# Seven-product matrix groups: two snapshots and a subtraction written ahead of the next group's parts, at high priority

## The chip, the cores and the metric

The kernel runs on one core of a Trainium2 chip. The metric is the device time of one execution in microseconds. The five engines of the core work at the same time, each through a queue of its own and in the order of that queue: PE (TensorE, matrix products, with its weight loads shown apart as PEld), DVE (VectorE), ACT (ScalarE), POOL (GpSimd, here mostly an issuer of transfers) and SP (an issuer of transfers). A difference of up to 0.3% is what a measurement of this kernel cannot tell from no change.

## The reference

Two layers, each with one norm, one wide input projection, three parallel mixers (a short convolution, stick-breaking attention, gated linear attention, GLA), a gate on each, and one output projection into the residual stream. `x` is 512 tokens by 2048.

```python
def _layer(x, norm_g, w_in, ...):
    h = _rmsnorm(x, norm_g)
    proj = h @ w_in                       # 2048 x 7696
    y_conv = _short_conv(cv_h, cv_b, cv_c, conv_w, conv_b) * silu(cv_g)
    y_sb = _stick_breaking(q, k, v) * silu(sb_g)
    y_gla = _rmsnorm(_gla(gl_q, gl_k, gl_v, g), gla_on_g) * silu(gl_g)
    mix = concatenate([y_conv, y_sb, y_gla])
    return x + mix @ w_out                # 2048 x 2048
```

## The kernel before

**Groups of 256 columns.** The weights of both projections are taken in 76 groups of 256 columns, in a fixed order (`specs`). A group is loaded into a staging tile `st` (two of them), its scale is found from squares (ACT, L383, then POOL, L399), and it is split into a high and a low half-precision part: ACT writes the high part `wh` (L507 or L454), DVE writes the low part `wl` (L508 or L461). A product of two split numbers is three half-precision products: high by high, high by low, low by high.

**Seven products instead of eight.** 42 of the groups are "quick": `wsums` (L512 on) cuts the group's weights into two by two blocks, forms sums of blocks, and splits seven of them (the last has the names `w7h`, `w7l`). `project_quick` then needs seven block products instead of eight, a Strassen scheme of Winograd's form. The seven products (`prod`, each 24 matmuls of 128x256 where the result has columns of the projection in partitions, L793, or 48 of 128x128 where it has tokens in partitions, L796) accumulate in four half banks `pa`, `pb`, `pd`, `pf`. Some accumulators are read in the middle of the work: `pa` is copied to `y12` after the first product (ACT, L808) and goes on accumulating with the fifth; `pb` minus that copy goes to `y21` (DVE, L809) before `pb` takes the sixth; `pd` is copied to `y22` (ACT, L812) before the seventh. These three readings are called the first snapshot, the first subtraction and the second snapshot here. The product that next writes the accumulator waits for its reading, and PE's queue is in order, so all of PE waits with it.

**Who sets the order.** ACT and DVE carry, beside the readings, the splits of the *next* group, the elementwise work of attention and GLA, and the squares of the group after. A scheduler of the framework lays out each engine's queue ahead of time, from the order in which the code is written and from a time line of its own; work inside `tc.high_priority()` is preferred to other ready work. The splits of the next group are made by `hook(...)`, which calls `parts_of` (L487 on), and `parts_of` runs inside `tc.high_priority()`. `hook` is called after the second product. The readings have no such mark, so a ready split is preferred to a ready reading.

**Staging.** The load of the group after next into a staging tile (POOL, L362) waits until the last split of the tile's old group, `w7l`, is made on DVE.

Of the kernel before, what the change touches and what calls it, by code (L numbers as in the profile page):

```python
# [10 lines left out]
AF = mybir.ActivationFunctionType  # L11
ALU = mybir.AluOpType
# [31 lines left out]
def hybrid_trunk(ctx, tc, x, norm_g, w_in, conv_w, conv_b, sb_qn_g, sb_kn_g,  # L44
                 gla_w_up, gla_b_up, gla_on_g, w_out, out):
    nc = tc.nc
    V, S, G, T = nc.vector, nc.scalar, nc.gpsimd, nc.tensor
# [27 lines left out]
    def sm(n, tag, bufs=None):  # L75
        return small.tile([P, n], F32, tag=tag, name=nm(tag), bufs=bufs or 1 + (tag in TWICE))
# [7 lines left out]
    def bank(pool, tag):  # L84
        return pool.tile([P, 512], F32, tag=tag, name=nm("ps" + tag))
# [402 lines left out]
    def hook(mm):  # L488

        if hooks:  # L490
            hooks.pop(0)(mm)
# [44 lines left out]
    def weights():  # L536

        i = cursor[0]
        cursor[0] += 1
        held = names[i][:2] == "v " or names[i] == "conv h 1"  # L540
        if i + 2 < len(specs) and not held:
            with tc.high_priority():
                fetch(i + 2)
        assert not hooks

        def first(mm):
            squares(i + 1, mm)
            if held:
                with tc.high_priority():
                    fetch(i + 2, added[0])  # L550

        if i and i + 1 < len(specs):
            hooks.extend([first, lambda mm: parts_of(i + 1, mm)])
        return loaded.pop(i)
# [130 lines left out]
    for l in range(depth):  # L685
# [92 lines left out]
        def project_quick(src, sums, y, cols):  # L778

            (w11, wT2, w22, wT3, w21, wt1, wT4), u = weights()  # L780
            (pa, pb), (pd, pf) = ([bk[:, n * GW:(n + 1) * GW] for n in range(2)]
                                  for bk in [bank(psp, "p") for _ in range(2)])
            a11, a12, a22 = ([a[:, 2 * r:2 * r + 2, c::2, :] for a in src] for r, c in ((0, 0), (0, 1), (1, 1)))
            s_, a21_22, a12_s, a11_21 = sums

            def prod(o, w, a, start, stop=False):
                for t in range(1 if cols else 2):
                    for kk in range(HK):
                        for i, (p_, q_) in enumerate(((0, 0), (0, 1), (1, 0))):
                            st_ = start and t == kk == i == 0  # L790
                            en = stop and kk == HK - 1 and i == 2
                            if cols:
                                mm = T.matmul(o, w[q_][:, kk, :], a[p_][:, :, kk, :], start=st_, stop=en,  # L793
                                              skip_group_check=True)
                            else:
                                mm = T.matmul(o[:, t * P:(t + 1) * P], a[p_][:, t, kk, :], w[q_][:, kk, :], start=st_,  # L796
                                              stop=en, skip_group_check=True)
                            if start and t == kk == 0 and i == 2 and o is pa:
                                hook(mm)
                return mm  # L800

            y11, y12, y21, y22 = (
                y[:, c, r * GW:(r + 1) * GW] if cols else y[:, 2 * r:2 * r + 2, c * P:(c + 1) * P]
                for r in range(2) for c in range(2))
            za, zb, zd, zf = (a if cols else a.rearrange("p (t c) -> p t c", c=P) for a in (pa, pb, pd, pf))
            prod(pa, w11, a11, True)
            hook(prod(pb, wT2, s_, False))
            S.activation(y12, za, AF.Copy)  # L808
            V.tensor_tensor(y21, zb, y12, ALU.subtract)  # L809
            prod(pf, w22, a12_s, True)  # L810
            prod(pd, wT3, a11_21, False)
            S.activation(y22, zd, AF.Copy)  # L812
            prod(pa, w21, a12, False)
            prod(pb, wt1, a21_22, False, True)
            S.activation(y11, za, AF.Copy)
            V.tensor_tensor(y12, zb, y12, ALU.subtract)
            V.tensor_tensor(y22, y12, y22, ALU.subtract)
            lastmm[0] = prod(pd, wT4, a22, False, True)
            V.tensor_tensor(y12, zf, y12, ALU.add)
            yield 0, u  # L820
            V.tensor_tensor(y21, zd, y21, ALU.subtract)
            yield 2, u
# [70 lines left out]
        def mixscale(j, m, tag, top=11.0):  # L893

            pow2(pmix[:, j:j + 1], m, -top, tag)
            s_ = sm(1, tag + "smix")
            V.reciprocal(s_, pmix[:, j:j + 1])
            return s_
# [103 lines left out]
        for tag in ("qT", "kT"):  # L1002
# [10 lines left out]
            s_ = sm(1, "gas")  # L1013
# [300 lines left out]
        for j in range(4):  # L1314
# [17 lines left out]
            s_ = mixscale(2 + j, m, "b", 12.0)  # L1332
# [141 lines left out]
```

## Time and profile before

| what | value |
|---|---|
| median of 3 runs | 1646.34 us (1645.41 to 1650.85) |
| profiled execution | 1652.09 us, of which the span of the profile is 1650.3 us |
| PE busy | 1624.0 us (98%) |
| DVE busy | 1418.1 us (86%) |
| ACT busy | 1184.7 us (72%) |
| weight loads (PEld) busy | 1342.5 us (81%) |
| POOL busy | 265.8 us (16%) |

A row of a time line has the start, the time (both in us), the engine, the line of the kernel, the operation, and `out<-in` by the names of the tiles; in brackets stands the idle time of the engine before it and what ended it. In the view of waits a row has the total, the number of times and the longest. A matmul's shown time is from its issue to a modelled end, and matmuls overlap, so the pace of PE is read from starts.

### The profile page before, as it was taken

The numbers are of one execution on the slowest core, as the hardware profiler recorded it, in microseconds if no ns is written. First come the engines' busy times: TensorE is split into PE (matmuls) and PEld (weight loads), VectorE is DVE, ScalarE is ACT, GpSimd is POOL, SyncE is SP. The second block draws the span as 40 slices with busy tenths as digits, with TensorE's granted clock in tenths as the row PEclk, the third lists the DMA queues.
The fourth block names the chain that finished last, engine by engine and source line by source line (L and its number), as shares of the span: only waits on it lengthen the run. The fifth ranks groups of instructions, "written<-read, shape, count | busy, mean of one in ns | idle before, by whom it ended". The sixth has DMA issues, their size and how long they took to land.

```text
span 1650.3 us, 41605 instructions
## 1 busy us (share of the span) xinstructions
PE 1624.0 (98%) x17914; PEld 1342.5 (81%) x17914; DVE 1418.1 (86%) x2377; ACT 1184.7 (72%) x1743; POOL 265.8 (16%) x298
## 2 busy tenths in 40 slices
PE   8999999999999999999999999999999999999999
PEld 6746668989999967799986468689898989668998
DVE  7977989989898978898699689898898889888893
ACT  7667887877777776756766687787777768666571
POOL 0121011111112121111112011221121111211110
PEclk9999999999999999999999999999999999999999
DMA  7144334486768687544633344445776886894441
GB/s 259 54 146 127 73 113 100 116 161 149 166 148 167 148 167 207 161 154 150 204 110 116 103 116 112 132 94 137 152 157 153 151 163 152 165 189 157 154 155 53
DMA packets 193913, 234.90 MB, mean 142 GB/s; under 512 B 90226, under 2 KB 154044, under 8 KB 193216
## 3 DMA queue, kind: packets, MB, share of 16 engines
q0 software_dynamic: 76992, 177.22, 40.5%
q1 hardware_dynamic: 107728, 45.56, 14.5%
q10 hardware_dynamic: 9008, 9.45, 1.7%
q8 instruction: 140, 2.29, 0.6%
q14 instruction: 45, 0.37, 0.1%
HBM read 179.65 MB, written 14.68 MB: 118 GB/s over the span
## 4 chain that ended last, share of the span: by engine, by line
PE 37%; DVE 6%; DMA 4%; ACT 2%; issue 1%; POOL 0%; SPq 0%; DVEq 0%; ACTq 0%; POOLq 0%
PE psp L796 10%; PE psp L793 6%; PE psp L843 5%; PE psp L712 3%; PE psp L714 3%; PE psp L713 3%; PE psp L701 2%; PE psp L702 2%; PE psp L703 2%; DMA st<-in_w_in_dram 2%; DVE wl L508 1%; DMA m<-mixd 1%; DMA th<-za 1%; DVE za L1280 1%; DMA kT<-raw 1%
## 5 line engine op out<-in xcount | busy, mean ns | idle before, releaser
L507 ACT ACTIVATE wh<-st,ws 128x1024 f16<-128x1024 f32 x252 | 280.8, 1145 | 174.5 <-DVE st L527 92.0
L508 DVE SCALAR_TENSOR_TENSOR wl<-st,ws,wh 128x1024 f16<-128x1024 f32 x252 | 316.7, 1278 | 31.1 <-ACT wh L507 31.0
L383 ACT ACTIVATE junk<-st 128x2048 uint8<-128x2048 f32 x150 | 285.4, 1903 | 17.9 <-DMA st<-in_w_in_dram 8.8
L793 PE MATMUL psp<-s,wh 128*128 128x256 f16 x1152 | 195.6, 273 | 0.0
L793 PEld LDWEIGHTS <-wh 128*128 128x128 f16 x1728 | 168.3, 98 | 21.5 <-issue 1.3
L796 PE MATMUL psp<-wh,s 128*128 128x128 f16 x2048 | 176.9, 219 | 1.9 <-issue 1.9
L714 PE MATMUL psp<-wh,m 128*128 128x256 f16 x640 | 174.5, 273 | 1.2 <-DVE m L1189 1.2
L712 PE MATMUL psp<-wh,m 128*128 128x256 f16 x640 | 174.5, 273 | 0.2 <-issue 0.2
L796 PEld LDWEIGHTS <-s 128*128 128x128 f16 x3072 | 172.9, 98 | 2.0 <-issue 2.0
L713 PE MATMUL psp<-wl,m 128*128 128x256 f16 x640 | 174.5, 273 | 0.0
L796 PE MATMUL psp<-wl,s 128*128 128x128 f16 x1024 | 173.2, 219 | 0.0
L461 DVE SCALAR_TENSOR_TENSOR wl<-st,ws,wh 128x2048 f16<-128x2048 f32 x68 | 158.9, 2346 | 14.6 <-ACT wh L454 13.8
L454 ACT ACTIVATE wh<-st,ws 128x2048 f16<-128x2048 f32 x66 | 130.5, 1995 | 40.7 <-DVE ws L415 22.6
L362 POOL DMA_DIRECT2D st<-in_w_in_dram x114 | 109.8, 1029 | 297.8 <-DVE w7l L508 110.7
L793 PE MATMUL psp<-s,wl 128*128 128x256 f16 x576 | 156.7, 273 | 0.0
L796 PEld LDWEIGHTS <-m 128*128 128x128 f16 x2304 | 131.1, 98 | 2.7 <-issue 2.2
L399 POOL PARTITION_ALL_REDUCE wgm<-wm x75 | 55.5, 740 | 482.5 <-ACT junk L383 469.4
L386 POOL DMA_DIRECT2D st<-st x34 | 54.0, 1589 | 307.2 <-ACT junk L383 266.8
L793 PEld LDWEIGHTS <-wl 128*128 128x128 f16 x864 | 84.5, 98 | 13.4 <-issue 3.4
L796 PE MATMUL psp<-wh,m 128*128 128x128 f16 x1024 | 91.5, 219 | 0.4 <-DVE kT L809 0.4
L796 PE MATMUL psp<-wl,m 128*128 128x128 f16 x512 | 87.5, 219 | 0.0
L703 PEld LDWEIGHTS <-wl 128*128 128x128 f16 x448 | 43.8, 98 | 53.6 <-DVE wl L461 2.3
(442 smaller groups left out, 4199.8 us busy)
## 6 DMA issues: line engine op xcount, KB each, us to landing
st<-in_w_in_dram POOLq DMA_DIRECT2D x114, 1024.0 KB, 8.3
st<-in_w_out_dram POOLq DMA_DIRECT2D x32, 1024.0 KB, 8.5
st<-st POOLq DMA_DIRECT2D x34, 512.0 KB, 6.8
st<-in_w_in_dram SPq DMA_DIRECT2D x6, 1024.0 KB, 12.0
mixd<-g POOLq DMA_DIRECT2D x20, 256.0 KB, 7.9
x<-in_x_dram SPq DMA_DIRECT2D x4, 1024.0 KB, 4.9
qT<-in_x_dram ACTq DMA_DIRECT2D x8, 512.0 KB, 6.2
qT<-xs ACTq DMA_DIRECT2D x8, 512.0 KB, 4.0
```

The lines of the kernel that those rows point to most:

```text
L362: load = queue.dma_start(s_, src[l, h * HK * P:(h + 1) * HK * P, c0:c0 + GW].rearrange("(k p) n -> p k n", p=P), max_dma_last_dim=1024)
L383: sq = S.activation(junk(HK * GW).rearrange("p (k n) -> p k n", k=part.shape[1]), part, AF.Square, accum_out=peak[i][:, h:h + 1])
L454: hi = S.activation(wh[:, :, :GW], staged[i][h], AF.Copy, scale=scales[i])
L461: V.scalar_tensor_tensor(wl[:, :, :GW], staged[i][h], scales[i], wh[:, :, :GW], ALU.mult, ALU.subtract)
L507: hi = S.activation(h_, b, AF.Copy, scale=sc)
L508: V.scalar_tensor_tensor(l_, b, sc, h_, ALU.mult, ALU.subtract)
L712: T.matmul(o, ah[:, t, k, :], wh[:, kk, :n], start=st_, stop=False, skip_group_check=True)
L713: T.matmul(o, ah[:, t, k, :], wl[:, kk, :n], start=False, stop=False, skip_group_check=True)
L714: return T.matmul(o, al[:, t, k, :], wh[:, kk, :n], start=False, stop=en, skip_group_check=True)
L793: mm = T.matmul(o, w[q_][:, kk, :], a[p_][:, :, kk, :], start=st_, stop=en, skip_group_check=True)
L796: mm = T.matmul(o[:, t * P:(t + 1) * P], a[p_][:, t, kk, :], w[q_][:, kk, :], start=st_, stop=en, skip_group_check=True)
L843: mm = T.matmul(o[:, :n], a_[:, t, k, :], w[k // HK][part][:, k % HK, :n], start=i == 0 and k == 0, stop=i == 2 and k == KT - 1)
```

## The change

The second product's last matmul is kept in a variable. The first snapshot and the first subtraction are put inside `tc.high_priority()` and written ahead of `hook`, so that they stand ahead of the next group's splits both by mark and by place. The second snapshot gets the mark and stays where it is written. No instruction is added or taken away, and no tile changes its size.

```diff
             prod(pa, w11, a11, True)
-            hook(prod(pb, wT2, s_, False))
-            S.activation(y12, za, AF.Copy)
-            V.tensor_tensor(y21, zb, y12, ALU.subtract)
+            mm = prod(pb, wT2, s_, False)
+            with tc.high_priority():
+                S.activation(y12, za, AF.Copy)
+                V.tensor_tensor(y21, zb, y12, ALU.subtract)
+            hook(mm)
             prod(pf, w22, a12_s, True)
             prod(pd, wT3, a11_21, False)
-            S.activation(y22, zd, AF.Copy)
+            with tc.high_priority():
+                S.activation(y22, zd, AF.Copy)
             prod(pa, w21, a12, False)
             prod(pb, wt1, a21_22, False, True)
             S.activation(y11, za, AF.Copy)
```

What the scheduler makes of it is seen in the queues. In the changed program the lines behind the edit are 3 higher; L808, L809 and L812 are now L809, L810 and L815. The queues of POOL and SP are the same. Three places follow.

**ACT, the key group of an attention pair in layer 1** (`kT` is the group's result, `raw` the result of the group before, `wh` the high part of the next group's weights). Before:

```order
L454 ACTIVATE wh_20687<-st_20136,ws_20683 128x8x256
L912 ACTIVATE g_18412<-e_20548,bsmix_18648 128x512
L1377 ACTIVATE qp_20541<-raw_20135 128x1024
L454 ACTIVATE wh_20691<-st_20136,ws_20683 128x8x256
L812 ACTIVATE kT_20571<-psp_20576 128x2x128
L815 ACTIVATE kT_20571<-psp_20575 128x2x128
```

Now:

```order
L454 ACTIVATE wh_20689<-st_20136,ws_20685 128x8x256
L915 ACTIVATE g_18412<-e_20548,bsmix_18648 128x512
L1380 ACTIVATE qp_20541<-raw_20135 128x1024
L815 ACTIVATE kT_20571<-psp_20576 128x2x128
L454 ACTIVATE wh_20693<-st_20136,ws_20685 128x8x256
L818 ACTIVATE kT_20571<-psp_20575 128x2x128
```

The second snapshot has changed places with one split of the next group. In 40 of the 42 quick groups the second snapshot has gone ahead of at least one split in this way (of 128x1024 or 128x2048). The first snapshot is moved forward in 6 of the 42, moved backward in 2, and stands where it stood in 34.

**DVE, the first gate group of the attention while the second half of GLA is worked off, layer 1** (`g` is the gate group's result; `zw`, `qp`, `th` and `e` belong to GLA; `wl` and `w7l` are low parts of weights). Before:

```order
L1105 COPY_PREDICATED zw_14223<-mdiag,own_14488 128x1024
L809 TENSOR_TENSOR g_15623<-psp_15627,g_15623 128x256
L415 TENSOR_SCALAR ws_15688<-wq_15683 128x1
L417 TENSOR_SCALAR wu_15690<-wq_15683,inoff_158 128x1
L508 SCALAR_TENSOR_TENSOR w7l_15453<-st_15239,ws_15442,w7h_15452 128x1024
L1038 TENSOR_TENSOR qp_13072<-e_14491,qp_13072 128x256
L1044 TENSOR_TENSOR th_13073<-e_14491,th_13073 128x256
```

Now:

```order
L1041 TENSOR_TENSOR qp_13072<-e_14491,qp_13072 128x256
L1047 TENSOR_TENSOR th_13073<-e_14491,th_13073 128x256
L1041 TENSOR_TENSOR qp_13072<-e_14504,qp_13072 128x256
L532 TENSOR_TENSOR st_15239<-st_15239 128x8x128
L1047 TENSOR_TENSOR th_13073<-e_14504,th_13073 128x256
L1128 SCALAR_TENSOR_TENSOR th_13074<-zw_14223,th_13074 128x256
L402 TENSOR_TENSOR wq_15685<-wgm_15686 128x1
L1128 SCALAR_TENSOR_TENSOR th_13074<-zw_14223,th_13074 128x256 x3
L810 TENSOR_TENSOR g_15623<-psp_15627,g_15623 128x256
L411 TENSOR_SCALAR wq_15685<-wq_15685 128x1
L508 SCALAR_TENSOR_TENSOR w7l_15453<-st_15239,ws_15442,w7h_15452 128x1024
```

Here the first subtraction and `w7l` now stand behind two L1038, two L1044 and four L1125 of GLA (L1041, L1047 and L1128 in the changed program). On PE some of GLA's small products (L1051) likewise stand earlier among those of the gate group. Layer 0 has the same in its own copy of this section.

**DVE, the end of the first query group, layer 1** (`raw` is its result, `kT` that of the key group behind it). Before:

```order
L821 TENSOR_TENSOR raw_15863<-psp_15868,raw_15863 128x2x128
L1166 SCALAR_TENSOR_TENSOR za_15012<-za_15012,par,g_13573 128x512
L411 TENSOR_SCALAR wq_16382<-wq_16382 128x1
L191 TENSOR_SCALAR pmix_12517<-bpc_15855 128x1
L508 SCALAR_TENSOR_TENSOR w7l_15987<-st_15624,ws_15976,w7h_15986 128x1024
L809 TENSOR_TENSOR kT_16275<-psp_16279,kT_16275 128x2x128
L415 TENSOR_SCALAR ws_16387<-wq_16382 128x1
```

Now:

```order
L411 TENSOR_SCALAR wq_16384<-wq_16384 128x1
L824 TENSOR_TENSOR raw_15863<-psp_15868,raw_15863 128x2x128
L508 SCALAR_TENSOR_TENSOR w7l_15989<-st_15624,ws_15978,w7h_15988 128x1024
L810 TENSOR_TENSOR kT_16275<-psp_16279,kT_16275 128x2x128
L1169 SCALAR_TENSOR_TENSOR za_15012<-za_15012,par,g_13573 128x512
L191 TENSOR_SCALAR pmix_12517<-bpc_15855 128x1
L415 TENSOR_SCALAR ws_16389<-wq_16384 128x1
```

`w7l` and the first subtraction of the key group have gone ahead of L1166 (a GLA scaling) and L191. Layer 0 has the same.

## The prediction

> **What bounds the kernel now.** I read the page first, then the chain of waits, then the view of waits of PE alone. The page's head:
>
> ```profile
> span 1650.3 us, 41605 instructions
> PE 1624.0 (98%) x17914; PEld 1342.5 (81%) x17914; DVE 1418.1 (86%) x2377; ACT 1184.7 (72%) x1743; POOL 265.8 (16%) x298
> ```
>
> PE is idle for 1650.3 - 1624.0 = 26.3 us, and no reordering of ACT and DVE can take more than that from the span, unless busy PE hides stalls. So the pace within busy stretches comes next, from the chain of waits (start, us, engine, tile, line, count):
>
> ```profile
> 946.67 10.48 PE psp L793 x96
> ...
> 1201.19 27.01 PE psp L796 x480
> ...
> 1550.69 75.04 PE psp L796 x1344
> ```
>
> 10.48/96 is 109 ns for a matmul of 128x256; 27.01/480 is 56.3 ns and 75.04/1344 is 55.8 ns for one of 128x128. Long stretches in different layers and at different neighbours have one pace, so PE is streaming there and nothing is hidden. The kernel is bound by PE, and what counts is who makes it stop. Its waits:
>
> ```profile
> PE psp L793 <- DVE zw L809: 3.1, 2, 1.6
> ...
> PE psp L793 <- DVE w7l L508: 2.0, 2, 1.1
> PE psp L796 <- issue: 1.9, 1, 1.9
> PE psz L1264 <- DMA kT<-raw: 1.4, 3, 0.5
> ...
> PE psp L796 <- DVE kT L809: 0.4, 1, 0.4
> PE psp L793 <- ACT g L812: 0.4, 1, 0.4
> PE psp L796 <- ACT kT L812: 0.4, 1, 0.4
> ```
>
> The readings that the change moves (L808, L809, L812) stop PE for 3.1 + 0.4 + 0.4 + 0.4 = 4.3 us; L808 never does, since the first subtraction comes after it. L508 and the transfer `kT<-raw` cost 3.4 us more, and the change moves some of them too. The field of play is small: 4.3 us is 0.26% of the span.
>
> **The change part by part.** Nothing is added or removed, so each term is a stall that goes or comes.
>
> *Second snapshot.* It goes ahead of one split in 40 groups, so it is earlier by one split (1.15 us of 128x1024 or 2.0 us of 128x2048) and the split is later by one snapshot (0.36 us). What that is worth is the stall there now. The key group of an attention pair in layer 1:
>
> ```profile
> 1393.29 1.99 ACT L454 ACTIVATE wh<-st,ws 128x2048 f16<-128x2048 f32 x1
> ...
> 1395.18 0.37 ACT L812 ACTIVATE kT<-psp 128x256 f32<-128x256 f32 x1
> ...
> 1395.44 0.22 PE L796 MATMUL psp<-wh,s 128*128 128x128 f16 x1
> ...
> 1395.60 0.22 PE L796 MATMUL psp<-w7h,m 128*128 128x128 f16 x1
> ```
>
> The seventh product begins right behind the snapshot's end (1395.55), 0.16 us behind the matmul before, where the pace is 0.056: a loss of 0.10 us. The view of waits does not list this, since the matmul before is still shown as running. I find the same in six key groups. Five lose 0.1 each, and the one of the wait row above 0.4 plus 0.1: 5 x 0.1 + 0.5 = 1.0 us. In the rest of the 40 groups PE comes to the seventh product 1.1 us or more after the snapshot, so being early there is worth nothing. The 0.4 us on `g L812` stays: that snapshot stands where it stood. I take 0.9 us. The 0.36 us by which a split is late is hidden by the products still to run on the old group's weights. The tightest case of a delayed split that I find:
>
> ```profile
> 1459.91 3.90 ACT L454 ACTIVATE wh<-st,ws 128x2048 f16<-128x2048 f32 x2 [5.08 <-DVE ws L415]
> ```
>
> ```profile
> 1463.79 0.38 PE L701 MATMUL psp<-m,wh 128*128 128x512 f16 x1
> ```
>
> The first of the two ends near 1461.9, 1.9 us before its first matmul, and it becomes 0.7 us later (an L912 has gone ahead of it). With this cover gone, 40 x 0.36 = 14 us would be lost, so this is the term to watch.
>
> *First snapshot and subtraction.* The largest wait, in the group that writes `zw` while GLA's first half is worked off:
>
> ```profile
> 1002.27 1.28 DVE L508 SCALAR_TENSOR_TENSOR w7l<-st,ws,w7h 128x1024 f16<-128x1024 f32 x1
> ...
> 1002.39 0.38 ACT L808 ACTIVATE zw<-psp 128x256 f32<-128x256 f32 x1 [0.32 <-DVE wq L411]
> ...
> 1003.65 0.42 DVE L809 TENSOR_TENSOR zw<-psp,zw 128x256 f32<-128x256 f32 x1
> ...
> 1004.12 0.27 PE L793 MATMUL psp<-m,wh 128*128 128x256 f16 x1 [1.48 <-DVE zw L809]
> ```
>
> The snapshot was released by DVE, not by PE: it writes into `zw`, which GLA's L1125 rows ahead of L411 were still reading. Priority cannot free a tile, `w7l` was ready first, and in the changed queue L508, L415, L417 and the subtraction stand there in the old order. The 3.1 us stay, in both layers. The 0.4 us on `kT L809` stays too, since no row around it moves.
>
> *GLA's second half (second place shown).* This speaks against the change. Two L1038, two L1044 and four L1125 now stand ahead of the subtraction:
>
> ```profile
> 1090.26 1.30 DVE L1105 COPY_PREDICATED zw<-mdiag,own 128x1024 f32<-128x1024 uint8 x1
> 1091.46 0.40 DVE L809 TENSOR_TENSOR g<-psp,g 128x256 f32<-128x256 f32 x1
> ...
> 1093.16 0.41 DVE L1038 TENSOR_TENSOR qp<-e,qp 128x256 f16<-128x256 f32 x1
> ...
> 1094.50 0.41 DVE L1125 SCALAR_TENSOR_TENSOR th<-zw,th 128x256 f16<-128x256 f32 x1
> ...
> 1095.08 1.08 DVE L1125 SCALAR_TENSOR_TENSOR th<-zw,th 128x256 f16<-128x256 f32 x3
> ```
>
> ```profile
> 1093.15 0.28 PE L793 MATMUL psp<-m,wh 128*128 128x256 f16 x1
> ```
>
> ```profile
> 1095.84 0.93 PE psz L1051 x20
> ```
>
> By starts the moved rows take (1094.50 - 1093.16) + (1096.09 - 1094.50) - 0.24 for two scalars between = 2.7 us; by summed durations 8 x 0.41 - 0.14 = 3.1. The subtraction, done at 1091.86, would be done at 1094.5 or 1095.0. PE wants it at 1093.15, and about 0.8 us later when most of those twenty L1051 stand ahead of it: 1093.95. That is a stall of 0.6 to 1.05 us, and a little more in layer 0, where I find 0.9 to 1.4. The lower bound is nothing: the same rows were brought forward because their inputs come earlier, and if DVE fills idle time the subtraction moves less. Bounds 0 and 2.45 us for both layers; I take 1.3, nearer to the row of starts, since that is how DVE ran here. `w7l` is late by as much and with it the load of the group after next; what covers that is the idle time of ACT and POOL in the groups that follow.
>
> *End of the first query group (third place).* `w7l` goes ahead of L1166 and L191. It has a chain behind it:
>
> ```profile
> 1134.38 0.74 DVE L1166 SCALAR_TENSOR_TENSOR za<-za,par,g 128x512 f32<-128x512 f32 x1
> ...
> 1136.73 1.79 POOL L362 DMA_DIRECT2D st<-in_w_in_dram  x2 [3.46 <-DVE w7l L508]
> ```
>
> ```profile
> 1146.96 1.91 ACT L383 ACTIVATE junk<-st 128x2048 uint8<-128x2048 f32 x1 [0.60 <-DMA st<-in_w_in_dram]
> ```
>
> ```profile
> 1166.46 0.38 PE L1264 MATMUL psz<-kT,qT 128*128 128x512 f16 x1 [0.48 <-DMA kT<-raw]
> 1167.28 0.59 PE L1264 MATMUL psz<-kT,qT 128*128 128x512 f16 x2 [0.45 <-DMA kT<-raw]
> ```
>
> `w7l` releases the load, the landing releases the squares on ACT, behind them in ACT's queue stand the key norms, and their result is transposed by the transfer that PE waits for. An earlier `w7l` (0.74 us) moves the load as much, but the squares only by the 0.60 us that ACT idles. Gain: 0 to 0.6 us per layer, and the waits of 1.4 us in all are enough to take it up. The subtraction of the key group also waits behind this `w7l`, with 0.1 us of loss in each layer. I take 0.4 + 0.1 per layer, 1.0 us.
>
> **The sum.** -0.9 + 1.3 - 1.0 = -0.6 us against the profiled 1652.09 us (span 1650.3 and 1.8 around it): 1651.5. The profiled execution stands 5.75 us above the median of the runs; the 1.9 us on `issue` is one stall that no other group of the kind shows. Against the median: 1646.34 - 0.6 = 1645.7 us. With each term at its bound the sum runs from -1.0 - 1.4 = -2.4 (1.4 is two layers of 0.6 + 0.1) to +2.45, so 1643.9 to 1648.8.
>
> **The rivals.**
>
> *All readings stop costing.* If the mark also frees the rows that I found unmoved (say that the splits ahead of them end sooner), the 4.3 us of wait rows, the hidden 0.6 of key groups and the 1.4 on `kT<-raw` go: 6.3 us, 1640.0 us. For it: the stalls exist, and six of them are touched. Against: 3.1 of them hang on the tile `zw`, and the queue there is the same.
>
> *GLA's second half starves the groups behind it: slower.* One mechanism: `w7l` in that section is 3.1 us later, the load it releases lands 3.1 us later, and the squares and splits of the following groups slide by it in full up to `kT<-raw`, where PE has no slack. Price 3.1 x 2 layers = 6.2, less 0.9 on key groups: +5.3, 1651.6 us. It decides where ACT and DVE have less idle time than 3.1 us between 1094 and 1135. For it: DVE is 86% busy, and its rows around 1088 to 1096 follow each other without idle time. Against: POOL is idle for 3.46 us ahead of the load at 1136.73, and that load waits for a `w7l` that has moved forward.
>
> *The change does nothing that PE notices.* The first snapshot stands unmoved in 34 groups, and the second had over a microsecond to spare in most: 1646.3 us. For it: DVE rows that moved forward may just wait longer for their inputs.
>
> *PE is not the bound.* Were busy PE full of hidden stalls, 40 snapshots earlier by 1.15 us at least would give up to 46 us, 1600 us. Against: the one pace of 55.8 to 56.3 ns above. The Trainium skill (Perfetto Trace Analysis, section Identifying the Most-Contended Engine) says that busy time of matmuls is a poor measure of headroom and that the busy share of weight loads is better. By that the 81% of PEld would leave a fifth of the span open. The trace decides against it here: the weight load runs beside the stream of a matmul, and the starts are evenly spaced.
>
> **How the numbers follow.** Chances: the sum as worked out, 0.66; nothing that PE notices, 0.14; all readings free, 0.11; starvation, 0.08; PE not the bound, 0.01. A difference under 0.3% (4.9 us) cannot be told from no change here. Faster by more needs a time under 1641.4: the third case and the last, 0.11 with what of the third falls short. Slower by more needs 1651.3: starvation, 0.08. The rest, 0.81, is within 0.3%. The range from 1641.0 to 1650.0 holds the two middle cases with a margin of one or two microseconds for the spread of single runs (the three before span 5.4 us), and cuts the far ends of the two outer ones.
>
> **What the changed profile would show.** The waits of PE on `kT L812` (in its new line) and the gaps of 0.16 us ahead of the key groups' seventh products are gone; 3.1 us on `zw` and the one on `g L812` stay. A new wait of PE on the first subtraction of `g` stands near 285 and 1093 us, of 0.5 to 1.4 us; if it is missing, my price for GLA is wrong. The waits of L1264 on `kT<-raw` are shorter by about half a microsecond per layer; if they are longer, starvation holds. PE's busy time stays at 1624 us within 2 us; a fall by more would show that stalls hid in it.

## The result, and the profile after

The changed kernel takes 1650.81 us (median of 19 runs, 1648.90 to 1656.78), the kernel before 1646.41 us beside it (19 runs, 1645.16 to 1650.85). The ratio is 1.0025 with a 95% interval of 1.0018 to 1.0032: 4.4 us slower, 3.0 to 5.3 by the interval. The forecast was 1645.7 us in a range of 1641.0 to 1650.0, so the sign and the size were missed. A loss of 0.25% is still within what the prediction called no change.

The head of the page after, and the waits of PE in the profiled execution of the changed kernel (total, times, longest; lines behind the edit are 3 higher):

```profile
span 1655.0 us, 41610 instructions
...
PE 1625.3 (98%) x17914; PEld 1343.5 (81%) x17914; DVE 1418.5 (86%) x2377; ACT 1184.8 (72%) x1743; POOL 261.8 (16%) x298
```

```profile
PE psp L796 <- DVE kT L810: 3.2, 3, 2.3
PE psp L793 <- DVE zw L810: 3.2, 2, 1.6
...
PE psp L703 <- DVE wl L461: 2.4, 3, 1.3
...
PE psz L1267 <- DMA kT<-raw: 2.1, 3, 1.1
...
PE psp L846 <- ACT wh L454: 1.5, 1, 1.5
...
PE psp L701 <- DVE lr L962: 0.8, 1, 0.8
```

PE's busy time has grown by 1.3 us (1624.0 to 1625.3) and the span by 4.7 us: the loss is PE standing still, as the prediction said any difference would be. But the rows are others than forecast. `kT L812` and `g L812` are gone from the list, `zw` is unchanged, and there is no row for the first subtraction of `g`. In their place stand `wl L461` three times instead of once, `wh L454` at 1.5 instead of 1.0, `lr L962`, which the list of before doesn't have at all, and `kT L810` at 3.2 us.

Both profiled executions stand 6 us above the median of their kernel, so both kernels were profiled once more (the experiments e4 and e15 below). These two calmer executions are the better pair. Before:

```profile
core 0 of [0], span 1644.4 us
...
PE psp L703 <- DVE wl L461: 1.3, 1, 1.3
...
PE psz L1264 <- DMA kT<-raw: 1.1, 2, 0.7
PE psp L843 <- ACT wh L454: 1.0, 1, 1.0
```

After:

```profile
core 0 of [0], span 1649.5 us
...
PE psp L703 <- DVE wl L461: 2.4, 3, 1.3
...
PE psp L846 <- ACT wh L454: 1.5, 1, 1.5
PE psz L1267 <- DMA kT<-raw: 1.3, 2, 0.9
...
PE psp L701 <- DVE lr L962: 0.8, 1, 0.8
PE psp L796 <- DVE kT L810: 0.8, 2, 0.4
```

The 2.3 us on `kT L810` are missing here, so they were one event of one execution. The other new rows stay. To find what each is worth, I took the start of the same matmul (by its place in PE's order) in two profiles and watched where the difference makes a step. The kernel before of e4 is the reference throughout; GLA's small products stand in another order on PE, so I read the difference only where the order is the same. The steps that recur:

| place | first matmul behind it, us in e4 | step in the changed kernel (e15) |
|---|---|---|
| key group behind GLA, both layers | 329 and 1135 | +0.42 and +0.47 |
| group conv b 1 (second convolution part), both layers | 652 and 1460 | +0.66 and +0.66 |
| first weights of layer 1 | 812 | +0.45 |
| GLA's decay rates, layer 1 | 893 | +1.02 |
| six key groups, ahead of the seventh product | 416 to 1391 | -0.1 each |
| first gate group of the attention, at the first subtraction of `g`, both layers | 288 and 1095 | +0.46 and +0.47 |
| GLA's small products (L1051), five places at which they stand in other blocks | 157 to 1065 | -0.2 each |
| two small places | 642 and 999 | +0.13 and +0.07 |

The first five rows add up to 0.89 + 1.32 + 0.45 + 1.02 - 0.6 = 3.1 us of the 4.4. The last three nearly cancel: 0.93 - 1.05 + 0.20 = 0.1 us.

### The profile page after: what moved, and what is told of

It reads as the page before. It is cut to its first block, busy times and chain, and to the rows that moved or that the text cites. A ratio compares the mean times of both kernels' runs of the same rounds, so it can differ in the third digit from the quotient of the medians.

```text
span 1655.0 us, 41610 instructions
## 1 busy us (share of the span) xinstructions
PE 1625.3 (98%) x17914; PEld 1343.5 (81%) x17914; DVE 1418.5 (86%) x2377; ACT 1184.8 (72%) x1743; POOL 261.8 (16%) x298
## 4 chain that ended last, share of the span: by engine, by line
PE 32%; DVE 10%; DMA 3%; ACT 3%; issue 2%; POOL 1%; SPq 0%; DVEq 0%; POOLq 0%; ACTq 0%
PE psp L796 10%; PE psp L793 5%; PE psp L846 4%; PE psp L714 2%; PE psp L712 2%; PE psp L713 2%; DVE wl L508 2%; PE psp L701 2%; PE psp L702 2%; PE psp L703 2%; DMA st<-in_w_in_dram 1%; DMA m<-mixd 1%; ACT junk L383 1%; DVE wl L461 1%; DVE zw L1089 1%
## 5 line engine op out<-in xcount | busy, mean ns | idle before, releaser
L383 ACT ACTIVATE junk<-st 128x2048 uint8<-128x2048 f32 x150 | 285.5, 1903 | 20.6 <-DMA st<-in_w_out_dram 10.3
L461 DVE SCALAR_TENSOR_TENSOR wl<-st,ws,wh 128x2048 f16<-128x2048 f32 x68 | 159.1, 2347 | 20.1 <-ACT wh L454 19.3
L454 ACT ACTIVATE wh<-st,ws 128x2048 f16<-128x2048 f32 x66 | 131.1, 1995 | 35.6 <-DVE ws L415 24.0
L399 POOL PARTITION_ALL_REDUCE wgm<-wm x75 | 52.0, 693 | 462.9 <-ACT junk L383 448.0
## 6 DMA issues: line engine op xcount, KB each, us to landing
st<-in_w_in_dram SPq DMA_DIRECT2D x6, 1024.0 KB, 11.9
```

Of the source, the lines that this page charges most:

```text
L383: sq = S.activation(junk(HK * GW).rearrange("p (k n) -> p k n", k=part.shape[1]), part, AF.Square, accum_out=peak[i][:, h:h + 1])
L454: hi = S.activation(wh[:, :, :GW], staged[i][h], AF.Copy, scale=scales[i])
L461: V.scalar_tensor_tensor(wl[:, :, :GW], staged[i][h], scales[i], wh[:, :, :GW], ALU.mult, ALU.subtract)
```

## The experiments

**Which part of the change does it.** The change has two parts, the first snapshot with its subtraction, and the second snapshot. e1 makes the first alone, e2 the second alone.

```diff
-            hook(prod(pb, wT2, s_, False))
-            S.activation(y12, za, AF.Copy)
-            V.tensor_tensor(y21, zb, y12, ALU.subtract)
+            mm = prod(pb, wT2, s_, False)
+            with tc.high_priority():
+                S.activation(y12, za, AF.Copy)
+                V.tensor_tensor(y21, zb, y12, ALU.subtract)
+            hook(mm)
```

> Only the first snapshot and the first subtraction are marked and written ahead; the second snapshot is left as before. In the queues six subtractions and four first snapshots move by one row each, nothing else. Theory A (the mark on the second snapshot makes the whole difference): 1646.4 us, ratio 1.000, PE's waits as before (wl L461 one of 1.3, kT L809 0.4). Theory B (what stands ahead of the splits after the second product delays them): the whole loss is here, 1650.8 us, ratio 1.0025, and wl L461 is waited for three times.

Measured: 1648.17 us, ratio 1.0006 (0.9996 to 1.0017), span 1644.5 us beside 1644.4 of e4, `wl L461` one wait of 1.3 us. No loss that can be told, and none of the new rows.

```diff
-            S.activation(y22, zd, AF.Copy)
+            with tc.high_priority(): S.activation(y22, zd, AF.Copy)
```

> Only the second snapshot is marked. Theory A: 1650.8 us, ratio 1.0025 (1.0015 to 1.0035), with the waits of the changed kernel: kT first subtraction 3 times and about 3.2 us, wl L461 3 times and about 2.4 us, kT<-raw about 2.1 us. Theory B: 1646 us or below, with the gain of 0.9 us of the key groups and no new wait.

Measured: 1650.63 us (the median of 12 runs, of which two lie far off, at 1857 and 6495 us), ratio 1.0024 (1.0012 to 1.0036), with `wl L461` 2.4 in three waits, `lr L959` 0.8, `wh L454` 1.5, and `kT L809` 0.9 in two. That is the changed kernel: theory A holds. Only the size of `kT` was off, by the event of the first profile. In the queues the two differ from each other by 4 rows on DVE and 2 on ACT; so the second snapshot's mark moves nearly all of what the change moves (618 rows on PE, 152 on DVE, 101 on ACT), though it is an instruction of 0.36 us that needs to pass one row.

**The key groups alone.** The term that the prediction was surest of.

```diff
-            S.activation(y22, zd, AF.Copy)
+            with tc.high_priority() if names[cursor[0] - 1][:2] == 'k ' else contextlib.nullcontext(): S.activation(y22, zd, AF.Copy)
```

> The second snapshot is marked in the eight key groups alone; in the queues eight snapshots change places with one split each, nothing else moves. My price of this term: the gaps of 0.16 us ahead of the seventh products and the wait on kT L812 go, 0.9 us, so 1645.5 us, ratio 0.9995. Rival (a split that is later by a snapshot costs as much wherever it happens): 8 x 0.36 = 2.9 us, 1649.3 us, ratio 1.0018, with new waits on wh or wl of the groups behind.

Measured: 1646.02 us, ratio 0.9995 (0.9986 to 1.0004). The snapshot is ahead of the split in the place that the prediction quoted:

```profile
1388.79 0.38 ACT L812 ACTIVATE kT<-psp 128x256 f32<-128x256 f32 x1
1389.05 2.01 ACT L454 ACTIVATE wh<-st,ws 128x2048 f16<-128x2048 f32 x1
```

All six gaps of 0.16 us are gone from PE, and nothing comes in their place; the eight later splits cost nothing. So the mechanism is right, the rival of 2.9 us is out, and the gain is 6 x 0.1 = 0.6 us, too small for the times to show it (the ratio's interval holds 1).

**The kernel before, once more.** No edit.

> The kernel before, profiled once more. If the 1.9 us that PE lost to issue at 1301.86 was one event of one execution, it is missing here, and the stall in front of the key group's wait on kT stands there in one piece of 2.4 to 2.7 us; whether PE then runs at half pace behind it, as in the changed kernel at 1310, shows if the 1.6 us of half pace belong to the change. If it belongs to the kernel, the row on issue is there again with 1.9 us and the pace behind it is full.

Measured: 1646.22 us, span 1644.4. The row on `issue`, the 0.4 us on `kT L809` and the 0.4 us on `kT L812` are all missing, and no stall of 2.4 us stands in their place. So three rows of the profile that the prediction was built on belong to that one execution. What differs beside them is a late load, seen in the issues of transfers (KB each, median us from issue to landing): in the first profile of before

```profile
st<-in_w_in_dram POOLq DMA_DIRECT2D x2, 1024.0 KB, 13.8
```

and in e4 for the same load

```profile
st<-in_w_in_dram POOLq DMA_DIRECT2D x2, 1024.0 KB, 9.0
```

The squares of that load (ACT, L383 at 1301.29 us) had to wait 1.99 us for it, and the two rows of 0.4 us stand behind them. What PE waits for in the row on `issue`, the profile doesn't show.

**Family by family.** With the condition of e3 changed, the mark was given to one kind of group at a time.

e5: `names[cursor[0] - 1][:2] == 'q '`

> The second snapshot is marked in the eight query groups alone. The end of the first query group stands on DVE as in the changed kernel (w7l ahead of L1166), on PE nothing moves. My price of this place: an earlier load, 0.4 us less on kT<-raw and 0.1 us less ahead of the key group, in each layer: 1.0 us faster, 1645.3 us. Theory S (a mark costs where a split or a subtraction that has no slack is made later): the key group's first subtraction kT L809, released now by DVE without loss near 328 and 1135 us, comes 0.4 to 0.5 us late in both layers, and kT<-raw gets longer by 0.4 to 0.6 us in both: 1.6 to 2.2 us slower, 1648.2 us.

Measured: 1647.46 us, ratio 1.0007 (0.9994 to 1.0019), span 1644.6. Theory S didn't happen: there is no wait on `kT L809`. Of my price, the 0.1 us ahead of the key group did go (steps of -0.13 us at 329 and at 1135); the 0.4 us on `kT<-raw` didn't (1.2 us beside 1.1). By itself an earlier `w7l` there costs nothing.

e6: `names[cursor[0] - 1] in ('conv c 0', 'conv g 0', 'gla gate 1')`

> The second snapshot is marked in the groups of the first convolution part and in the second gate group of GLA alone: of the 618 rows that the change moves on PE and the 152 on DVE, this moves 548 and 79, GLA's small products and its rows on DVE. My price: 1.3 us more, with a new wait of PE on the first subtraction of g of 0.5 to 1.4 us near 285 and 1093 us: 1647.6 us. Theory S: no split or subtraction of these groups loses its slack, so no new wait, within 0.3 us of before: 1646.4 us.

Measured: 1649.83 us, ratio 1.0016 (1.0004 to 1.0028), span 1645.0. The wait on the first subtraction of `g` is missing from the list, against my price; the starts of PE do show a loss there, of about 0.25 us in each layer (see the point on GLA's second half below). And a new row stands one group later, against theory S as well:

```profile
PE psz L1264 <- DMA kT<-raw: 1.9, 3, 1.2
...
PE psp L796 <- DVE raw L816: 0.6, 2, 0.3
```

e7: `names[cursor[0] - 1] in ('conv c 1', 'conv g 1')`

> The second snapshot is marked in the two quick groups of the second convolution part alone (four snapshots in all). My price: nothing, the split L454 has 1.9 us of cover: 1646.4 us. Theory S: wl L461 stands behind wh and had no cover; L912 ahead of two L454 makes it 0.7 us late, so PE's waits on wl L461 go from one of 1.3 us to three of 2.4 to 2.7 us, 1.1 to 1.4 us slower: 1647.7 us.

Measured: 1649.06 us, ratio 1.0015 (1.0004 to 1.0027), `wl L461` 2.4 us in three waits, PE later by 0.65 us at 652 and by 0.66 us at 1460. The place and the size of theory S hold; why `wl` is late is settled further down.

e8: `names[cursor[0] - 1].isdigit()`

> The second snapshot is marked in the quick groups of the output projection alone (eight snapshots). My price: nothing, 1646.4 us. Theory S: the first split L454 of layer 1 stands behind the snapshot of the last quick group of layer 0, wh L454 is waited for 1.4 instead of 1.0 us near 813 us, and DVE reaches lr L959 0.8 us later near 893 us: 1.2 us slower, 1647.6 us.

Measured: 1648.45 us, ratio 1.0014 (1.0004 to 1.0023); steps of 0.45 us at 812 and 1.01 us at 893, `wh L454` 1.5 and `lr L959` 0.8. The time lines show both chains. ACT, at the last quick group of layer 0:

```profile
803.64 0.39 ACT L812 ACTIVATE g<-psp 128x256 f32<-128x256 f32 x1 [0.29 <-PE psp L796]
803.92 1.48 ACT L1414 ACTIVATE junk<-x 128x1536 uint8<-128x1536 f32 x1
...
811.08 3.90 ACT L454 ACTIVATE wh<-st,ws 128x2048 f16<-128x2048 f32 x2 [1.20 <-DVE ws L415]
```

The snapshot now stands ahead of the last squares of `x` (L1414), where ACT has to stand still 0.29 us for PE. The squares of the weights (L383), their scale and the split come 0.65 us later than in e4, where the split starts at 810.43. Of that, 0.20 us is PE's own lateness in this execution by then; the other 0.45 us, mostly the 0.29 us of standing still, reach PE. On DVE the rows of the next layer's norm stand in another order, and between 841 and 864 us, where DVE has no idle time in e4, it now waits twice:

```profile
DVE wgm L401 <- POOL wgm L399: 0.5, 1, 0.5
DVE xrt L209 <- ACT xr L205: 0.3, 1, 0.3
```

0.8 us of idle time in a stretch in which DVE is 99% busy are never made good, and PE meets them at 894.28 (the wait of 0.85 us on `lr L959`).

The four ratios of e5 to e8 and that of e3 add up to more than that of the whole, but each is uncertain by about 0.0012. The steps add up but for 0.5 us at the key group behind GLA, where two families act together (e11).

**Ten snapshots against thirty.** Building the mark for one group name at a time shows, in the queues alone, that most marks change places with one row and do nothing else. Five names carry all the far moves: conv g 0, GLA's second gate group, the first query group, conv c 1 and output group 3. e9 marks these (two layers, ten snapshots), e10 all others but conv c 0. The queues of e9 differ from those of e2 by 27 rows on ACT, those of e10 from the kernel before by 27 rows on ACT, and by nothing else.

e9: `names[cursor[0] - 1] in ('conv g 0', 'gla gate 1', 'q 0', 'conv c 1', '3')`

> The second snapshot is marked in ten groups alone (per layer conv g 0, GLA's second gate group, the first query group, conv c 1, output group 3). In the queues this makes every move of the fully marked kernel but 27 single swaps on ACT: 618 rows on PE, 152 on DVE, 74 of 101 on ACT. Theory S (the loss comes from rows far from the snapshot, which the scheduler's time line carries along): the whole loss and not the gain of the key groups, 1646.5 + 4.2 + 0.6 = 1651 us, ratio 1.0024 to 1.0032, with waits on wl L461 of 2.4 us, lr L959 0.8, wh L454 1.5, kT first subtraction 0.9. Rival (each delayed split costs its share): 10 of 42 marks, 1647.5 us.

Measured: 1652.33 us, ratio 1.0028 (1.0017 to 1.0039), `wl L461` 2.4, `kT L809` 1.8 in three, `wh L454` 1.5, `lr L959` 0.8.

e10: `names[cursor[0] - 1] not in ('conv c 0', 'conv g 0', 'gla gate 1', 'q 0', 'conv c 1', '3')`

> The second snapshot is marked in thirty groups alone, all but those ten and the two conv c 0. In the queues 27 snapshots change places with one row on ACT, nothing else moves on any engine. Theory S: only the six gaps ahead of the key groups' seventh products go, 0.6 us, so 1645.9 us, ratio 0.9990 to 1.0003, and no new wait on wl, wh, lr or kT. Rival (each delayed split costs its share): 30 of 42 marks, 1649.5 us, ratio 1.0018.

Measured: 1648.62 us, ratio 1.0005 (0.9982 to 1.0029), a spread (1644.8 to 1661.5) in which the times alone decide little. The trace decides: no gap ahead of a key group's seventh product, and

```profile
PE psp L703 <- DVE wl L461: 1.3, 1, 1.3
...
PE psp L843 <- ACT wh L454: 1.1, 1, 1.1
```

with no row on `lr` or on `kT L809`, and steps of 0.01 us at most at the six places of loss. The loss is in the ten, and in rows that stand far from the snapshots that are marked: output group 3 disturbs the start of the next layer three groups later, conv c 1 the group conv b 1.

**Query groups and GLA together.** e6's row on `raw` and the changed kernel's row on `kT` are at the same place.

e11: the condition of e5 or that of e6.

> The marks of the query groups, of the first convolution part and of GLA's gate group together. Alone, the query groups gave no new wait, the others 0.3 us twice on raw L816 near 323 and 1129 us. If DVE's lateness out of GLA and w7l ahead of L1166 act together (starvation), the wait moves to kT L809, 0.4 to 0.5 us in each layer near 328 and 1136 us, 0.9 in all, as in the fully marked kernel. If they are independent, raw L816 stays at 0.6 and kT L809 is missing.

Measured: 1648.63 us in one run, and the rows

```profile
PE psp L796 <- DVE kT L809: 0.9, 2, 0.4
```

with no row on `raw L816`. The two act together. DVE in layer 1:

```profile
1134.51 0.42 DVE L819 TENSOR_TENSOR raw<-psp,raw 128x256 f32<-128x256 f32 x1
...
1135.29 1.28 DVE L508 SCALAR_TENSOR_TENSOR w7l<-st,ws,w7h 128x1024 f16<-128x1024 f32 x1
1136.49 0.42 DVE L809 TENSOR_TENSOR kT<-psp,kT 128x256 f32<-128x256 f32 x1
```

In e4 L819 stands at 1131.79 and the subtraction at 1134.43. Here they are 2.7 and 2.1 us later while PE is 1.6 us later: DVE comes out of GLA's second half late, and the query group's row order wins back only part of it.

**What makes `wl` late in conv b 1.** Two attempts missed. e12 made ACT later.

```diff
             S.activation(y22, zd, AF.Copy)
+            for _ in range({"conv g 1": 1 if cursor[0] < 40 else 3}.get(names[cursor[0] - 1], 0)): S.activation(y22, zd, AF.Copy)
```

> The kernel before, with the second snapshot of the group conv g 1 copied again, once more in layer 0 and three times more in layer 1, ahead of the two splits L454 whose low parts L461 PE waits for; no other row moves on ACT or DVE. A copy takes 0.27 us by starts. My price (1.9 us of cover behind L454): nothing, wl L461 one wait of 1.3 us as before. Theory S (wl stands behind wh, and its cover is zero): PE's first L703 near 652 us comes 0.27 us later and that near 1460 us 0.8 us later, wl L461 three waits, 2.2 to 2.4 us in all.

Measured: 1648.52 us in one run; `wl L461` one wait of 1.3 us, as before. Theory S in this form is wrong, and my price of the cover isn't tested, by this row:

```profile
1450.99 1.22 ACT L813 ACTIVATE g<-psp 128x256 f32<-128x256 f32 x3
1456.26 2.00 ACT L454 ACTIVATE wh<-st,ws 128x2048 f16<-128x2048 f32 x1 [4.05 <-DVE ws L415]
```

ACT stands idle 4.05 us ahead of the split, so the copies don't make it late: it starts 0.8 us later than in e4, where PE at that place is 1.2 us later. It is the scale `ws`, made on DVE, that the split waits for. So e13 and e14 made the scale late, by reductions ahead of it.

```diff
+        for _ in range((3, 5)[l] if names[i] == "conv b 1" else 0):
+            extra = V.tensor_reduce(u, staged[i][0][:, :2, :GW], AX.XY, ALU.max)
+            order(extra, first)
         V.tensor_scalar(sc.bitcast(I32), m.bitcast(I32), -1.0, ...
```

> The kernel before, with reductions over 128x512 of the staged weights written ahead of the scale ws (L415 before, here 4 lines lower) of the group conv b 1: three in layer 0, five in layer 1; by the scheduler one or two rows of 0.66 us change sides of ws too. Theory D (ws on DVE, then wh on ACT, then wl on DVE, then PE: no cover anywhere in this chain): PE's wait on wl near 652 and near 1460 us grows by what ws is late, about 1.1 to 1.3 us in layer 0 and 3.5 to 4.3 us in layer 1. Rival (1.9 us of cover behind the split on ACT): 0 and 1.6 to 2.4 us. The pace of PE behind the two stalls: if 2.5 us of standing still is enough for half pace, it halves for some 3.4 us behind the longer one and not behind the shorter.

> As the run before it, with four reductions in layer 0 and six in layer 1; a third row L1215 and an L1308 stand ahead of ws in layer 0, and an L913 in layer 1. Theory D: waits on wl of about 3.0 to 3.7 us and 5 us or more. Rival: 1 to 2 and 3 us or more. Half pace behind both, if 2.5 us of standing still is enough; behind the second alone, if it takes 3.4 us and more.

Measured: 1664.06 and 1668.19 us, one run each. Neither theory's row appears; PE waits 13.3 and 14.1 us for the transposes of `th` instead:

```profile
PE psm L1309 <- DMA th<-za: 13.3, 2, 6.9
```

The edit has moved rows on PE too, which its expectation didn't look at. In e4 seventeen products of `th` (L1304, here L1309) stand behind the whole of conv b 1, from 671.82 us on; in e13 twelve of them stand behind its second matmul, and PE's queue waits with them until 658.30 us. The transposes themselves aren't issued later (the last one at 652.26 us, in e4 at 654.08). So the two runs tell nothing about the scale; they are one more case of rows that the scheduler moves far from an edit. e16 does it the other way round: in the changed kernel one order holds the gating row of attention (L1308, now L1311) behind the scale. The line of the edit that does it:

```diff
+                if made: order(e_, made.pop())
```

(`e_` is L1311, `made` holds the L415 of conv b 1.)

> The changed kernel with one order added in each layer: the gating L1308 of GLA-side attention (L1311 there) of the last pair stays behind the scale ws (L415) of the group conv b 1. The section on DVE and ACT then stands as in the kernel before, 24 rows on DVE and 8 on ACT go back; all else is as in the changed kernel. Theory D (an L1308 ahead of ws makes ws, wh, wl and PE late by its 0.66 us): the two new waits on wl L461 go, one of 1.3 us stays, and 1.3 us come back: 1649.5 us, ratio 1.0015 to 1.002. Rival (the wait has another cause, say the L912 that went ahead of L454 on ACT, or DVE late from earlier groups): wl L461 three waits of 2.4 us, 1650.8 us.

Measured: 1649.49 us, ratio 1.0013 (1.0003 to 1.0024), 0.0012 below the changed kernel's 1.0025. The two intervals overlap, so it is the trace that decides. The two waits are gone:

```profile
PE psp L703 <- DVE wl L461: 1.3, 1, 1.3
```

and PE has no step at 652 and at 1460. What stood there in the changed kernel, on DVE, ACT and PE:

```profile
1464.22 0.15 DVE L415 TENSOR_SCALAR ws<-wq 128x1 int32<-128x1 int32 x1
...
1466.44 2.35 DVE L461 SCALAR_TENSOR_TENSOR wl<-st,ws,wh 128x2048 f16<-128x2048 f32 x1 [1.29 <-ACT wh L454]
```

```profile
1463.68 0.72 ACT L915 ACTIVATE m<-e,bsmix 128x512 f16<-128x512 f32 x1 [5.23 <-DVE e L1311]
1464.40 3.90 ACT L454 ACTIVATE wh<-st,ws 128x2048 f16<-128x2048 f32 x2
```

```profile
1468.85 0.39 PE L703 MATMUL psp<-m,wl 128*128 128x512 f16 x1 [0.53 <-DVE wl L461]
```

And before, on DVE and PE:

```profile
1459.73 0.15 DVE L415 TENSOR_SCALAR ws<-wq 128x1 int32<-128x1 int32 x1
...
1459.91 0.74 DVE L1308 SCALAR_TENSOR_TENSOR e<-psm,vu,g 128x512 f32<-128x512 f32 x1
1460.57 0.74 DVE L1215 SCALAR_TENSOR_TENSOR kT<-raw,par,kT 128x510 f32<-128x510 f32 x1
1461.95 4.61 DVE L461 SCALAR_TENSOR_TENSOR wl<-st,ws,wh 128x2048 f16<-128x2048 f32 x2 [0.63 <-ACT wh L454]
```

```profile
1464.22 0.27 PE L1304 MATMUL psm<-th,v 128*128 128x256 f16 x1
1464.35 0.39 PE L703 MATMUL psp<-m,wl 128*128 128x512 f16 x1
```

Before, `wl`'s first piece was done at about 1461.95 + 2.35 = 1464.30, and PE began to use it at 1464.35: no cover. With L1308 ahead of the scale, scale, split and `wl` come 0.66 us later, the distance of 1459.91 to 1460.57. What stays open: in the changed kernel the scale's end (1464.37) and the end of L915 (1464.40) both stand right ahead of the split, and both hang on L1311; e16 moves both back, so it isn't shown which would have been enough.

**The changed kernel, once more.** No edit.

> The changed kernel, profiled once more. If the 2.3 us on kT near 1309 us and the half pace behind it came from a load that landed late in that one execution (13.6 us behind its issue, where other executions show 7.5 to 9.1), they are missing here: span 1648 to 1649 us, the granted clock 1.00 in 1300 to 1320 us, and the other waits stay: wl L461 2.4, lr L962 0.8, wh L454 1.5, kT L810 0.9, kT<-raw 1.5 to 2. If they belong to the change, they are here again, with a span of 1652 us or more.

Measured: 1651.28 us, span 1649.5, its waits shown with the result. The 2.3 us and the half pace are missing, the rest stays. A row on `issue` of 1.1 us near 490 us isn't in the other profiles of the change; e10 has one of 1.6 us at the same matmul.

## Why the prediction was wrong, point by point

**What bounds the kernel: right.** PE's busy time changed by 1.3 us, and the places found are stalls of PE, but for some 0.2 us wherever the blocks of L1051 differ. Nothing speaks for the rival that PE is not the bound. Nor does anything here bear out the rule of the Trainium skill that was set against it (Perfetto Trace Analysis, section Identifying the Most-Contended Engine): PEld went from 1342.5 to 1343.5 us, and no idle share of it turned into time.

**The second snapshot, -0.9: mechanism right, mis-sized.** 0.6 us by e3. The 0.4 us on `kT L812` that I added came from the late load of the one profile.

**"The 0.36 us by which a split is late is hidden": right, and not the question.** e3 and e10 make splits later without a cost. But the next sentence, on the tightest case, is the step that failed. I saw the L912 ahead of the two L454 in conv b 1, quoted the row, and priced it with 1.9 us between the split's end and its first matmul. That row says in its bracket that ACT had idled 5.08 us for `ws L415`, so the chain comes from DVE, and behind `wh` stands `wl` with 2.35 us, for which the cover is 1464.35 - 1464.30 us, zero. It cost 1.3 us instead of nothing (e7, e16).

**Rows that were moved far from the edit: missing from the sum.** My three places were those where rows of the mark's own groups change. The start of layer 1, where output group 3's mark has reordered some 25 rows on DVE, had no term. It cost 0.45 + 1.0 us (e8), and DVE's 99% busy share there was in the trace to be read.

**GLA's second half, +1.3: mechanism right, mis-sized, and more came one group later.** The first subtraction did move behind the L1125, and PE does wait for it, though the view of waits doesn't list it:

```profile
1095.75 0.42 DVE L810 TENSOR_TENSOR g<-psp,g 128x256 f32<-128x256 f32 x1
```

```profile
1095.88 0.27 PE L793 MATMUL psp<-s,wh 128*128 128x256 f16 x1
1096.23 0.27 PE L793 MATMUL psp<-m,wh 128*128 128x256 f16 x1
```

The subtraction ends at 1096.17 and PE uses it at 1096.23, 0.35 us behind the matmul before, where the pace is 0.11: a loss of 0.24 us, hidden like the gaps of the key groups. All seven profiles with GLA's rows moved have this gap, of 0.33 to 0.37 us, in both layers; the others have none. So the term is 0.5 us and not 1.3. Set against PE's lateness just ahead (1.6 us, by the same matmul near 1084 in e4), the subtraction is 2.7 us later than before, as I took it (2.7 to 3.1). But PE comes 1.3 us later by the L1051 that now stand ahead of it (I took 0.8); with the 1.29 us of cover that leaves some 0.2 us and not 0.6 to 1.05. The same twenty L1051, one block before and two now, cost 0.2 us more in each layer. All of this is 0.93 us for both layers in e15, and 1.05 us come back at the five places where L1051 stand in other blocks, mostly one in place of two; so in the sum GLA's own section is near zero. What I held against the rival of starvation, that idle time of the following groups covers it, is half wrong: DVE stays late up to the key group two groups later, for 0.4 to 0.5 us of PE in each layer (e11, and 0.3 in e6). That mechanism is the rival's; its price is 0.9 us and not 6.2.

**End of the first query group, -1.0: wrong but for its small part.** Alone it gives the 0.13 us per layer ahead of the key group (I took 0.1) and nothing on `kT<-raw` (e5). In the company of GLA's lateness, PE loses at the key group. `kT<-raw` varies between executions of the kernel before by as much as I wanted to gain (1.4 and 1.1 us in all), so 0.4 us per layer couldn't have been read from it.

**First snapshot, 0: right** by e1. The wait on `zw` stays at 3.0 to 3.2 us as forecast. That on `g L812` was to stay as well; it is off the list of the first profile after and 0.9 us in the second, but it also varies in the kernel before (0.4 and 0.8), so it tells nothing.

**The sum.** -0.6 + 1.3 (conv b 1) + 1.5 (layer 1) + 0.9 (key groups behind GLA) = 3.1 us; with 0.1 for GLA's own section and the two small places, and 0.2 to 0.4 on layer 1's `kT<-raw` (a step of 0.24 to 0.57 in all seven profiles with GLA's rows moved, and of -0.18 to 0.37 in the others, so not clear of their scatter) that is 3.4 to 3.6 us. The measured interval is 3.0 to 5.3; the last 0.9 us to the median have no place that recurs.

No version came out that is measurably faster than the kernel before. The mark in the key groups alone (e3) takes out 0.6 us by the trace, and its ratio of 0.9995 (0.9986 to 1.0004) can't be told from 1.

## What to carry to other kernels

A priority mark on one instruction is an input to the scheduler's whole time line: compare the full queues of every engine, and price each row that moved, not those near the edit. For a row that feeds PE, follow the chain to the last link before PE (scale, high part, low part) and read the cover there; the bracket of a row tells on which engine the chain really hangs. Profile the kernel before twice before building a sum of tenths of a microsecond on its stalls: here 2.7 us of rows (`issue` 1.9, `kT` 0.4 and 0.4) stood behind one late transfer and were gone in the second profile.

## What the hardware showed beside it

**Half pace behind a stall.** In the first profile of the changed kernel the late load (13.6 us from issue to landing) left PE idle for 2.30 us at 1309.11. One microsecond later the granted clock fell to half. PE by stretches (busy us, instructions, clock, DMA share, GB/s):

```profile
1306.00:1310.20 4.20, 1.90 (x34) 0.99 0.00 0
1310.20:1313.50 3.30, 3.30 (x34) 0.50 0.80 247
1313.50:1320.00 6.50, 6.50 (x110) 1.00 1.11 271
```

32 matmuls started 0.107 us apart instead of 0.056: 1.6 us on top of the stall. Behind the wait of 6.4 us in e13 the same is seen:

```profile
658.20:662.00 3.80, 3.70 (x16) 0.50 1.12 351
```

Behind 1.9 us on `issue` in the first profile of before, and 1.65 us on `kT` in e14, the clock stayed at 1.00. The length of a stall alone doesn't decide, though: the wait of 2.02 us at 195.94 us in e10 was followed by full pace, that of 1.95 us at 17.99 us in e11 by half. What decides shows in the clock's records. They come in pieces of 3.41 us or whole multiples of it, on one grid in each execution (1310.10 to 1313.51 us here, 656.29 to 663.11 in e13). PE's idle time added up in each piece of that grid, in all 18 profiles, parts them: at full clock, each piece with 1.87 us of idle time or more was followed by half pace, and none with 1.85 us or less was. The 2.02 us of e10 fell on both sides of a boundary, with 1.58 us in the fuller piece; the 2.30 us here fell into one. Why it is so, no run shows. The Trainium skill (TensorE: Matmul & The Clock Gate, section Why this matters for your kernels) advises against idle gaps above about 3 us between matmul bursts; the gap measured here was shorter and was followed by half pace all the same.

**A late load, and 3 to 4 us behind it.** The same kind of load took 13.8 and 13.6 us to land in the two first profiles and 9.0 in e4. That is where half to two thirds of the 6 us lies by which both stood above their medians: at 1301 to 1312 us PE lost 3.1 us against e4 in the one, and in the other 4.1 us against e15, with the half pace. In layer 0 the same kind of load, near 476 us, was late in e10 and e15: its later half took 13.2 and 12.6 us to land, in e4 11.9, and both have their row on `issue` behind it. So all three rows on `issue` of over 1 us stand behind a late load. It isn't a rule without exception: in the first profile after and in e14, halves that took 13.1 and 12.8 us there were followed by no stall.
